# A two-layer decoder trunk: lo parts of 98 weight pieces subtracted by GpSimd instead of VectorE, in a new order of instructions

## The chip, the cores and the metric

One core of a Trainium2 chip runs the whole program. The metric is the device time of one execution in microseconds; the median of several runs is given, and one further execution was taken by the hardware profiler. The engines are called as the profile calls them: PE (TensorE, matmuls), PEld (its weight loads), DVE (VectorE), ACT (ScalarE), POOL (GpSimd), SP (SyncE, which issues most DMAs).

## The reference

Two layers over a sequence of 512 rows of 1024 float32 channels. Each layer normalises its input, multiplies it by one wide matrix, runs two branches, and merges them:

```python
h = rmsnorm(x, norm_g)
proj = h @ w_in                  # aq ak av az bqk bv bi bf bo bz ga gb
# branch A: differential attention, 8 heads, two score maps of 64 columns a head
q, k = rope(rmsnorm(aq)), rope(rmsnorm(ak))
a = softmax(q0 k0) - lam * softmax(q1 k1)     # causal
oa = rmsnorm(a @ v) * (1 - lam_init) * silu(az);   ya = oa @ w_out_a
# branch B: mLSTM matrix memory, 8 heads, causal convolution on q and k
hb = rmsnorm(mlstm(q, k, v, gates)) * sigmoid(bo) * silu(bz);   yb = hb @ w_out_b
u = sigmoid(ga) * ya + sigmoid(gb) * yb
x = x + u @ w_o
```

All of it is float32 in and out.

## The kernel before, in words

**Numbers in two parts.** PE multiplies in a rounded format (`fp32r`). To keep float32 accuracy every operand is split in a hi part and a lo part: ACT copies the source into the rounded format (`wh`, hi), and DVE subtracts that from the source (`wl`, lo). A product is then three matmuls: hi by hi, hi by lo, lo by hi. `split` does this for everything, weights and activations.

**Pieces.** The weights come from memory in pieces of 128 x 1024 values, 512 KB, in the order of `TUNE["order"]`: 111 pieces a layer, 222 in all. `qk0` to `qk3`, `av`, `bv` are four pieces each, `az`, `ga`, `bqk`, `bo`, `bz`, `woa`, `gb`, `wob` one for each index, `gate` is a small one, and `wo` is 14 pieces of a multiplication with seven products instead of eight (some of its weights are sums, which DMAs issued by POOL add up). `load` issues a piece's DMA on SP into one of two buffers `wr`; `prep`, three pieces ahead of the matmuls, makes `wh` (ACT) and `wl` (DVE), three buffers each. A piece is 24 matmuls of 512 columns.

**The rest of the work** hangs on clock ticks between pieces. In the first part of a layer the projections alternate with attention: `qk_done` normalises and rotates q and k (tiles `sq`, `rot`, `qss`), `back` transposes them in groups of four on PE (`qkt`) and ACT and DVE read them out (`qs`, `ks`, `kl`, or `qk_0x`, `qk_2x`); `attn_head` makes scores (`sc`), maxima (`mx`), probabilities (`p`), their transposes (`ut`) and the product with v. Later come the mLSTM heads (`ml_head`: `ms`, `dd`, `num`, `den`). The sums over 128 partitions that the norms need are matmuls with a matrix of ones: two of them (hi and lo), or one where `fold` first adds the two halves of the partitions and stacks hi and lo; `foldA`, `foldM`, `foldD` list the heads that fold. `qsq` lists the tiles whose squares are summed by ACT in eight 64-wide instructions; the others take one 512-wide square and a `tensor_reduce` on DVE. The tiles `sc`, `qk`, `qkt`, `ut`, `av` (as a matmul's output), `num`, `den`, `msp` lie in PSUM, the others in SBUF.

**The order of issue** is planned. `Recorder` records every operation with its dependences instead of issuing it, and `schedule` then plans all five queues with a cost for each operation, latencies between engines, the free buffers and a key for each operation (when it is due, with offsets by tile name in `bias`). The program is issued in that order, and each engine works through its own queue in order. The numbers in `TUNE` (`margin`, `pemargin`, `wait`, `wdiff`, `drain`, `risk`, `late` and others) are the planner's weights; `attn`, `ml`, `gateA`, `gct`, `gls`, `m4` and `acl` set the ticks at which steps fall due. All operations are issued from one helper, so the profile shows them under one line, L439, and is read by tile names.

The planner's cost of a POOL operation, and the place in `prep` where the pieces are split:

```python
if eng == "POOL":
    return 1000.0 if fn == "dma_start" else 200.0 + n
...
elif i < TUNE["wsp"]:
    A.copy(wh, loaded[i])
    for hf in range(2):
        cs = slice(S * hf, S * hf + S)
        V.tensor_tensor(wl[:, cs], loaded[i][:, cs], wh[:, cs].bitcast(F32), ALU.subtract)
else:
    split(wh, wl, loaded[i])
```

Of the kernel before, what the change touches and what calls it, by code (L numbers as in the profile page):

```python
# [9 lines left out]
F32 = mybir.dt.float32  # L10
# [3 lines left out]
ALU = mybir.AluOpType  # L14
# [21 lines left out]

TUNE = {
    "order": (
# [4 lines left out]
    ),  # L43
    "qkt": 5,
    "gct": 14,
    "gls": 6,
    "glf": 12,
    "attn": (1, 5, 5, 8, 9, 10, 12, 16, 16, 19, 24),
    "a0": 23,
    "ap": 18,  # L50
    "a4": 10,
    "ml": (1, 9, 11, 12, 13, 28),
    "ahead": 3,
    "lc": 9,
    "slack": 4130.0,
    "margin": 60.0,
    "pemargin": 48.4,
    "wait": 333.1,
    "swpen": 99746.2,
    "smargin": 0.2,  # L60
    "pwait": 2.0,
    "wdiff": 5762.0,
    "wsp": 0,
    "kact": (0, 2),
    "qsq": (1, 3),
    "foldA": (2, 3, 5, 6),
    "foldM": (0, 1, 2, 3, 4, 7),
    "foldD": (0, 1, 3, 5, 6),
    "warm": 18,
    "start": 'x0 ct ng w0 x1 w1 x2 x3',  # L70
    "prods": 'P1 P5 P3 P6 P2 P7 P4',
    "acl": 14,
    "gateA": 7,
    "gateM": 4,
    "actp": (0, 1, 2, 3),
    "m0": 217,
    "mp": 15,
    "m4": 17,
    "slots": 20,
    "bias": {'av': 11500.0, 'msp_a': -4400.0, 'wl': 2550.0, 'wo': -3700.0, 'mk': 6300.0, 'woh': -4650.0, 'wob': -850.0, 'bv': 2450.0, 'ht': 4400.0, 'woa': -1700.0, 'taz': -5550.0, 'sbo': -8700.0, 'wh': 7950.0, 'ga': -3100.0, 'ulZ': 7100.0, 'gt': -2650.0, 'qs': -5450.0, 'rq': -4050.0, 'p': -850.0, 'uz': -2750.0, 'x': -1750.0, 'ua': 5400.0, 'sdh': -3800.0, 'fo_b': -3100.0, 'lneps': 3350.0, 'wo1_P': 14300.0, 'qkt': -450.0, 'ml': 1700.0, 'den': -1900.0, 'sq': 3050.0, 'ulA': 10450.0, 'uhY': 1850.0, 'wo0_P': -850.0, 'cv': -2300.0, 'ulB': 8050.0, 'ob': 1850.0, 'gw': -150.0, 'out_0_dram': -3650.0, 'qss': 3500.0, 'gb': 100.0, 'xr': 1400.0, 'x1d': 5100.0, 'sinv': 5300.0, 'msl_a': 2200.0, 'p5_wo': -4150.0, 'saz': 3700.0, 's1_wo': 550.0, 'hh': -2400.0, 'mql': 1750.0, 'ulY': 9700.0, 'msp_b': 1200.0, 'em': -6750.0, 'sbz': -4900.0, 'wr': -2400.0, 'xn': 3500.0, 'posi': -500.0, 'ms': 12650.0, 'rot': 1400.0, 'sums': -1100.0, 'wt0_wo': 2350.0, 'mq': 650.0, 'uy': 100.0, 'qt': 5650.0, 'msh_d': 1700.0, 'gf': 1850.0, 'warm': -1450.0, 'ctab': 4550.0, 'gct': -4200.0, 'hl': 150.0, 'fo_a': 350.0, 'ones': 2100.0, 'fb_a': -700.0, 'ut': 450.0, 'ld': 5350.0, 'ang': -1900.0, 'mx': 5650.0, 'dq': 2300.0, 'uh': -500.0, 'gm': -550.0, 'fb_d': 1400.0, 'zeroc': 6400.0, 'gft': -100.0, 'bqk': 2050.0, 'gcol': -1000.0, 'oa': 500.0, 'sdl': 4250.0, 'uhB': 5750.0, 'tbz': 1150.0, 'cosv': 500.0, 'sc': 150.0, 'gi': 6100.0, 'msh_a': 400.0, 'uhA': 250.0, 'ss': 400.0, 'bo': 2500.0, 'posf': 2100.0, 'eps': -6650.0, 'fo_d': -2950.0, 'ws0_wo': -200.0, 'msh_b': -350.0, 'qk0_2x': 150.0, 'msl_d': -3500.0, 'junk': -900.0, 'epsc': 3000.0, 'fb_b': -100.0, 'kl': 1100.0, 'ks': -1450.0, 'msl_b': 200.0, 'ng': 550.0, 'rows': 150.0, 'gc': -150.0, 'qk1_0x': -500.0, 'qk1_2x': 100.0, 'stab': 650.0},  # L80
    "drain": 689.4,
    "risk": 335.5,
    "late": 278.0,
}


# [16 lines left out]
class Recorder:  # L103
# [111 lines left out]
    @staticmethod  # L215
    def cost(eng, fn, a, k):
        def cols(ap):
            n = 1
            for x in list(ap.shape)[1:]:
                n *= x  # L220
            return n

        def ps(ap):
            return isinstance(ap, bass.AP) and ap.space == PSUM

        n = cols(a[0])
        if eng == "PE" and a[0].tensor.name.startswith("warm"):
            return 350.0
        if eng == "PE":
            n = cols(a[2]) if fn == "matmul" else cols(a[0])  # L230
            return max(n / 2.4 + 13.4, 107.5)
        if eng == "POOL":
            return 1000.0 if fn == "dma_start" else 200.0 + n
        if eng == "ACT":
            x = 52 + n * 0.833 + (0 if ps(a[1]) else 42)
            for v in (k.get("bias"), k.get("scale")):
                if isinstance(v, bass.AP):
                    x += 93
            if k.get("accum_out") is not None:
                x += 93  # L240
            return x
        if eng == "DVE":
            aps = [v for v in a[1:] if isinstance(v, bass.AP)]
            if fn == "reciprocal":
                return 64 + 6.26 * n
            if fn == "memset":
                return 8 + n * 1.04
            if fn == "tensor_reduce":
                return 69 + cols(a[1]) / 0.96
            if fn == "tensor_tensor_scan":  # L250
                return 69 + 2 * n / 0.96
            fast = fn in ("tensor_scalar", "tensor_copy") and not ps(a[1])
            x = 69 + (n / 1.92 if fast else n / 0.96)
            if fn in ("tensor_scalar", "scalar_tensor_tensor"):
                x += 61 * sum(1 for v in a[2:] if isinstance(v, bass.AP) and cols(v) == 1)
            return x
        return 400.0
# [185 lines left out]
def kernel(ctx, tc, x, pos, wp, wg, cst, par, pb, ngb, out):  # L443
    nc = tc.nc
    depth = wp.shape[0]
# [28 lines left out]
    V, A, T = rec.engine("DVE", nc.vector), rec.engine("ACT", nc.scalar), rec.engine("PE", nc.tensor)  # L474
    SY = rec.engine("SP", nc.sync)
    G = rec.engine("POOL", nc.gpsimd)

    def t2(name, dt=F32):
        return s2.tile([P, S], dt, tag="s2", name=name)
# [7 lines left out]
    def split(hi, lo, src):  # L487
        A.copy(hi, src)
        V.tensor_tensor(lo, src, hi.bitcast(F32), ALU.subtract)
# [9 lines left out]
    ct = cp.tile([P, C_N], F32, name="ct")  # L499
    posi = cp.tile([P, NT], I32, name="posi")  # L500
# [10 lines left out]
    ones = cp.tile([P, P], F32R, name="ones")  # L511
    V.memset(ones.bitcast(F32), 1.0)
    epsc = cp.tile([P, 1], F32, name="epsc")
# [3 lines left out]
    lneps = cp.tile([P, 1], F32, name="lneps")  # L517
    V.memset(lneps, math.log(EPS))
    zeroc = cp.tile([P, 1], F32, name="zeroc")
    V.memset(zeroc, 0.0)  # L520

    rows = dram.tile([16, S], F32, name="rows")


    if TUNE["warm"]:
        pw = ps_acc.tile([P, S], F32, tag="acc", name="warm")
        zw = t2("zw", F32R)
# [5 lines left out]
    cosv = cp.tile([P, NT, 32], F32, name="cosv")  # L533
    sinv = cp.tile([P, NT, 32], F32, name="sinv")
# [71 lines left out]
    def give(n):  # L606
        state["q2"] -= n
# [13 lines left out]
    x1d = dram.tile([S, D], F32, name="x1d")  # L621
# [833 lines left out]
    pieces = [(l, e[1]) for l in range(depth) for e in layers[l][0]]  # L1455
# [6 lines left out]
    loaded, ready = {}, {}  # L1462
# [46 lines left out]
    def prep(i):  # L1509
        if i >= len(pieces) or i in ready:  # L1510
            return
        load(i)
        l, key = pieces[i]
        if key == "gate":
            wh = wpool.tile([P, 1024], F32R, tag="wh", name=f"wh{i}")
            w4 = wh.rearrange("p (k a n) -> p k a n", k=KT, a=2)
            split(w4[:, :, 0, :], w4[:, :, 1, :], loaded[i][:, :512].rearrange("p (k n) -> p k n", k=KT))
            ready[i] = (wh, None)
            return
        wh = wpool.tile([P, 1024], F32R, tag="wh", name=f"wh{i}")  # L1520
        wl = wpool.tile([P, 1024], F32R, tag="wl", name=f"wl{i}")
        if key[0] == "seven" and key[2] in ("P5", "P6", "P7", "P4"):
            _, n, prod, a = key
            load_sums(i)
            t = chains[n, a, 3] if prod == "P7" else chains[n, a]
            split(wh, wl, t)
            if prod in ("P5", "P6"):
                add_up(l, n, "T2" if prod == "P5" else "T4", a)
            else:
                give(1)  # L1530
        elif i < TUNE["wsp"]:
            A.copy(wh, loaded[i])
            for hf in range(2):
                cs = slice(S * hf, S * hf + S)
                V.tensor_tensor(wl[:, cs], loaded[i][:, cs], wh[:, cs].bitcast(F32), ALU.subtract)
        else:
            split(wh, wl, loaded[i])
        ready[i] = (wh, wl)

    for n in TUNE["start"].split():  # L1540
# [4 lines left out]
        else:  # L1545
            SY.dma_start(ng0 if n == "ng" else ct, ngb[0] if n == "ng" else cst)
    late_loads()
    prep(0)
    for i, run in enumerate(runs):
        if i in starts:  # L1550
# [94 lines left out]
```

## Time and profile before

| | |
|---|---|
| median of 3 runs | 1344.44 us (1344.25 to 1344.85) |
| the profiled execution's own time | 1344.67 us |
| its span, first to last instruction | 1342.9 us |
| PE busy | 1331.3 us |
| DVE busy | 1012.6 us |
| ACT busy | 904.7 us |
| POOL busy | 36.9 us, 44 instructions |
| granted TensorE clock | 0.999 |

The span is shorter than the execution's time by what lies around it. Busy times of different engines overlap, so they don't add up; an engine that is busy nearly all of the span leaves little that the others could give back. Rows of groups read: line, engine, operation, output <- inputs, shapes, count, then total busy us, mean ns of one, and the idle time before them with what ended it. Rows of the time line read: start us, duration us, engine, operation, and the idle time before it in brackets. Layer 0 runs to about 673 us, layer 1 from there.

### The profile page before, as it was taken

What the parts mean: (1) busy time and instruction counts of PE and PEld (TensorE: products, weight loads), DVE (VectorE), ACT (ScalarE), POOL (GpSimd) and SP (SyncE); (2) the same over time, 40 slices, a digit from 0 to 9 for tenths busy, and PEclk for the clock granted to TensorE, in tenths of its full rate; (3) what the DMA queues carried; (4) which work ended last, traced back from release to release, by engine and by line L of the source; (5) the groups of instructions that cost most, each with busy time, mean ns of one, the idle gap of its engine ahead of it and who ended that gap; (6) DMA issues with size and microseconds to landing.
All of it is one profiled execution on the core that took longest, in us unless ns stands there. A gap on an engine that the chain in (4) does not pass through costs nothing.

```text
span 1342.9 us, 17724 instructions
## 1 busy us (share of the span) xinstructions
PE 1331.3 (99%) x6300; PEld 1100.0 (82%) x6300; DVE 1012.6 (75%) x1806; ACT 904.7 (67%) x1828; POOL 36.9 (3%) x44
## 2 busy tenths in 40 slices
PE   8999999999999999999999999999999999999998
PEld 7787878888888888888888888788888888888887
DVE  7888988786549958755888888887754698587386
ACT  5787888885438858733668787888743488586243
POOL 1000000000000000000200000000000000000010
PEclk9999999999999999999999999999999999999999
DMA  5222222323244433455933122222322434434366
GB/s 186 87 79 64 79 78 64 94 77 101 91 119 112 132 108 114 137 136 146 265 104 97 53 95 63 79 63 94 99 82 91 120 107 135 128 109 140 121 190 172
DMA packets 51274, 148.17 MB, mean 110 GB/s; under 512 B 6096, under 2 KB 12880, under 8 KB 51184
## 3 DMA queue, kind: packets, MB, share of 16 engines
q1 hardware_dynamic: 48880, 138.63, 33.7%
q0 software_dynamic: 2304, 8.39, 3.5%
q8 instruction: 50, 0.82, 0.3%
q14 instruction: 40, 0.33, 0.1%
HBM read 142.74 MB, written 4.26 MB: 109 GB/s over the span
## 4 chain that ended last, share of the span: by engine, by line
PE 98%; ACT 1%; DMA 0%; DVE 0%; issue 0%; SPq 0%; DVEq 0%
PE qk L439 13%; PE av L439 9%; PE az L439 7%; PE ga L439 7%; PE bv L439 7%; PE bo L439 7%; PE bz L439 7%; PE woa L439 7%; PE gb L439 7%; PE bqk L439 7%; PE wob L439 6%; PE wo_P L439 6%; PE sc L439 3%; PE num L439 2%; PE ms L439 1%; PE ut L439 1%
## 5 line engine op out<-in xcount | busy, mean ns | idle before, releaser
L439 ACT CAST wh<-wr 128x1024 fp32r<-128x1024 f32 (+1 forms) x206 | 214.9, 1045 | 195.8 <-PE woa L439 37.7
L439 DVE TENSOR_TENSOR wl<-wr,wh 128x1024 fp32r<-128x1024 f32 x204 | 249.0, 1221 | 108.5 <-ACT wh L439 105.7
L439 PE MATMUL qk<-wl,hh 128*128 128x512 f32 x256 | 94.1, 398 | 0.7 <-DVE wl L439 0.7
L439 PE MATMUL qk<-wh,hl 128*128 128x512 f32 x256 | 93.8, 400 | 0.1
L439 PE MATMUL qk<-wh,hh 128*128 128x512 f32 x256 | 93.3, 399 | 0.6 <-ACT hh L439 0.6
L439 PE MATMUL woa<-oa,wh 128*128 128x512 f32 x256 | 88.5, 391 | 0.0
L439 PE MATMUL wob<-ob,wh 128*128 128x512 f32 x256 | 83.4, 389 | 0.0
L439 ACT ACTIVATE p<-sc,mx,rq 128x128 f32<-128x128 f32 (+3 forms) x128 | 78.9, 618 | 6.5 <-DVE mx L439 6.0
L438 ACT ACT_TABLE_LOAD x61 | 78.3, 1283 | 1.1
L439 PEld LDWEIGHTS qk<-wl,hh 128*128 128x128 f32 x256 | 47.9, 188 | 10.6 <-DVE wl L439 1.2
L439 PEld LDWEIGHTS wob<-ob,wh 128*128 128x128 f32 x256 | 48.1, 188 | 10.0
L439 PEld LDWEIGHTS qk<-wh,hl 128*128 128x128 f32 x256 | 48.0, 188 | 9.7 <-DVE hl L439 0.4
L439 PEld LDWEIGHTS woa<-oa,wh 128*128 128x128 f32 x256 | 47.8, 188 | 9.7
L439 PEld LDWEIGHTS qk<-wh,hh 128*128 128x128 f32 x256 | 47.7, 188 | 9.5 <-ACT hh L439 0.9
L439 DVE TENSOR_REDUCE mx<-sc 128x2 f32<-128x256 f32 (+1 forms) x64 | 52.5, 821 | 0.9
L439 PE MATMUL az<-hh,wl 128*128 128x512 f32 x128 | 51.3, 401 | 0.0
L439 PE MATMUL az<-hl,wh 128*128 128x512 f32 x128 | 50.9, 398 | 0.0
L439 PE MATMUL ga<-hh,wl 128*128 128x512 f32 x128 | 50.6, 398 | 0.0
L439 PE MATMUL ga<-hh,wh 128*128 128x512 f32 x128 | 50.5, 395 | 0.0
L439 PE MATMUL az<-hh,wh 128*128 128x512 f32 x128 | 50.5, 397 | 0.0
L439 PE MATMUL ga<-hl,wh 128*128 128x512 f32 x128 | 50.4, 394 | 0.0
L439 PE MATMUL woa<-oa,wl 128*128 128x512 f32 x128 | 50.0, 391 | 0.0
(314 smaller groups left out, 3737.7 us busy)
## 6 DMA issues: line engine op xcount, KB each, us to landing
wr<-in_wp_dram SPq DMA_DIRECT2D x204, 512.0 KB, 3.6
ws_wo<-in_wp_dram POOLq DMA_DIRECT2D x12, 512.0 KB, 6.6
dd<-rows SPq DMA_DIRECT2D x16, 256.0 KB, 4.9
em<-rows SPq DMA_DIRECT2D x16, 256.0 KB, 3.9
dd<-rows SPq DMA_DIRECT2D x16, 192.0 KB, 5.4
x<-in_x_dram SPq DMA_DIRECT2D x4, 512.0 KB, 8.5
dd<-rows SPq DMA_DIRECT2D x16, 128.0 KB, 6.2
ws_wo<-in_wp_dram SPq DMA_DIRECT2D x4, 512.0 KB
```

What stands on the lines that cost most here:

```text
L438: self.tc.keep_in_program_order(self.nc.scalar.preload_act_table_set(self.SET_NAME[o["load"]]))
L439: self.tc.keep_in_program_order(getattr(o["e"], o["fn"])(*o["a"], **o["k"]))
```

## The change

`prep` gets a branch: pieces 3 to 52 of each layer (49 of them are not the gate piece, which is split elsewhere) are copied by ACT as before, but the subtraction is issued to POOL. The planner's cost for such an operation is raised. `wsp` 3 makes the first three pieces of layer 0 use the existing branch that subtracts in two halves. One more head folds in each of `foldA`, `foldM` and `foldD`, `qsq` keeps one tile of four, and `order`, the ticks, the planner's weights and the table `bias` (from 114 names to 103, most values changed; left out here) are other ones.

```diff
     "order": (
-        "qk0 av0 gate az0 qk1 az1 az2 av1 qk2 az3 az4 qk3 ga0 az6 ga7 az5 ga3 ga2 ga4 az7 bv0 woa3 woa4 "
-        "bqk7 woa2 ga6 bqk4 bqk1 ga5 bo0 woa6 bo1 woa7 ga1 bz1 bqk5 bqk0 woa5 bz0 woa1 bqk6 woa0 bqk2 "
-        "bo2 bz2 bo4 bz4 bo3 bv1 bz3 bo6 bo5 bz5 bqk3 bo7 bz7 bz6 gb2 gb0 wob2 wob0 gb3 gb4 wob3 gb1 "
-        "wob1 gb6 gb7 wob6 wob4 gb5 wob5 wob7 wo"
+        "qk0 av0 gate az0 qk1 az1 az2 av1 qk2 az3 az4 qk3 az6 ga0 ga3 az5 ga2 ga4 ga7 az7 bv0 woa3 ga6 "
+        "bo0 woa4 bqk0 woa2 bqk7 bqk1 woa6 ga1 ga5 bo1 woa5 bz1 bqk5 bqk4 woa7 bz0 woa1 bqk6 woa0 bo2 "
+        "bz2 bo4 bz4 bqk2 bo3 bv1 bz3 bo6 bo5 bz5 bqk3 bo7 bz7 bz6 gb0 gb2 wob0 gb4 gb3 gb7 wob2 wob3 "
+        "wob4 gb6 gb1 wob6 wob1 gb5 wob5 wob7 wo"
     ),
-    "gct": 14,
-    "gls": 6,
+    "gct": 15,
+    "gls": 7,
-    "attn": (1, 5, 5, 8, 9, 10, 12, 16, 16, 19, 24),
+    "attn": (1, 5, 5, 9, 9, 10, 12, 16, 16, 19, 24),
-    "ml": (1, 9, 11, 12, 13, 28),
+    "ml": (1, 9, 10, 12, 13, 28),
-    "margin": 60.0,
-    "pemargin": 48.4,
-    "wait": 333.1,
-    "swpen": 99746.2,
-    "smargin": 0.2,
-    "pwait": 2.0,
-    "wdiff": 5762.0,
-    "wsp": 0,
+    "margin": 21.4,
+    "pemargin": 225.8,
+    "wait": 383.3,
+    "swpen": 8658.5,
+    "smargin": 101.0,
+    "pwait": 0.3,
+    "wdiff": 9165.4,
+    "wsp": 3,
-    "qsq": (1, 3),
-    "foldA": (2, 3, 5, 6),
-    "foldM": (0, 1, 2, 3, 4, 7),
-    "foldD": (0, 1, 3, 5, 6),
+    "qsq": (3,),
+    "foldA": (0, 1, 2, 5, 6),
+    "foldM": (0, 1, 2, 3, 4, 5, 7),
+    "foldD": (0, 1, 3, 4, 5, 6),
-    "acl": 14,
-    "gateA": 7,
+    "plo": (3, 50),
+    "acl": 12,
+    "gateA": 0,
-    "m4": 17,
+    "m4": 20,
-    "drain": 689.4,
-    "risk": 335.5,
-    "late": 278.0,
+    "drain": 508.6,
+    "risk": 41.0,
+    "late": 93.2,
...
         if eng == "POOL":
-            return 1000.0 if fn == "dma_start" else 200.0 + n
+            return 1000.0 if fn == "dma_start" else 200.0 + n * (2.0 if fn == "tensor_tensor" else 1.0)
...
+        elif len(pieces) // depth * l <= i - TUNE["plo"][0] < len(pieces) // depth * l + TUNE["plo"][1]:
+            A.copy(wh, loaded[i])
+            G.tensor_tensor(wl, loaded[i], wh.bitcast(F32), ALU.subtract)
         else:
             split(wh, wl, loaded[i])
```

More of the change, by code (lines that the diff above doesn't have):

```diff
@@ L77 @@
     "mp": 15,
-    "m4": 17,
+    "m4": 20,
     "slots": 20,
-    "bias": {'av': 11500.0, 'msp_a': -4400.0, 'wl': 2550.0, 'wo': -3700.0, 'mk': 6300.0, 'woh': -4650.0, 'wob': -850.0, 'bv': 2450.0, 'ht': 4400.0, 'woa': -1700.0, 'taz': -5550.0, 'sbo': -8700.0, 'wh': 7950.0, 'ga': -3100.0, 'ulZ': 7100.0, 'gt': -2650.0, 'qs': -5450.0, 'rq': -4050.0, 'p': -850.0, 'uz': -2750.0, 'x': -1750.0, 'ua': 5400.0, 'sdh': -3800.0, 'fo_b': -3100.0, 'lneps': 3350.0, 'wo1_P': 14300.0, 'qkt': -450.0, 'ml': 1700.0, 'den': -1900.0, 'sq': 3050.0, 'ulA': 10450.0, 'uhY': 1850.0, 'wo0_P': -850.0, 'cv': -2300.0, 'ulB': 8050.0, 'ob': 1850.0, 'gw': -150.0, 'out_0_dram': -3650.0, 'qss': 3500.0, 'gb': 100.0, 'xr': 1400.0, 'x1d': 5100.0, 'sinv': 5300.0, 'msl_a': 2200.0, 'p5_wo': -4150.0, 'saz': 3700.0, 's1_wo': 550.0, 'hh': -2400.0, 'mql': 1750.0, 'ulY': 9700.0, 'msp_b': 1200.0, 'em': -6750.0, 'sbz': -4900.0, 'wr': -2400.0, 'xn': 3500.0, 'posi': -500.0, 'ms': 12650.0, 'rot': 1400.0, 'sums': -1100.0, 'wt0_wo': 2350.0, 'mq': 650.0, 'uy': 100.0, 'qt': 5650.0, 'msh_d': 1700.0, 'gf': 1850.0, 'warm': -1450.0, 'ctab': 4550.0, 'gct': -4200.0, 'hl': 150.0, 'fo_a': 350.0, 'ones': 2100.0, 'fb_a': -700.0, 'ut': 450.0, 'ld': 5350.0, 'ang': -1900.0, 'mx': 5650.0, 'dq': 2300.0, 'uh': -500.0, 'gm': -550.0, 'fb_d': 1400.0, 'zeroc': 6400.0, 'gft': -100.0, 'bqk': 2050.0, 'gcol': -1000.0, 'oa': 500.0, 'sdl': 4250.0, 'uhB': 5750.0, 'tbz': 1150.0, 'cosv': 500.0, 'sc': 150.0, 'gi': 6100.0, 'msh_a': 400.0, 'uhA': 250.0, 'ss': 400.0, 'bo': 2500.0, 'posf': 2100.0, 'eps': -6650.0, 'fo_d': -2950.0, 'ws0_wo': -200.0, 'msh_b': -350.0, 'qk0_2x': 150.0, 'msl_d': -3500.0, 'junk': -900.0, 'epsc': 3000.0, 'fb_b': -100.0, 'kl': 1100.0, 'ks': -1450.0, 'msl_b': 200.0, 'ng': 550.0, 'rows': 150.0, 'gc': -150.0, 'qk1_0x': -500.0, 'qk1_2x': 100.0, 'stab': 650.0},
@@ L81 @@
-    "drain": 689.4,
-    "risk": 335.5,
-    "late": 278.0,
+    "bias": {'av': 15250.0, 'msp_a': -4100.0, 'wl': 2450.0, 'wo': -3700.0, 'woh': -4650.0, 'bv': 1500.0, 'woa': -4550.0, 'taz': -5950.0, 'sbo': -8700.0, 'wh': 9300.0, 'ga': -6750.0, 'ulZ': 10000.0, 'rq': -4500.0, 'uz': -3450.0, 'wo1_P': 11050.0, 'wo0_P': -2800.0, 'cv': -1950.0, 'p5_wo': -7600.0, 'mql': 3900.0, 'dd': 7450.0, 'gi': 11550.0, 'uy': 650.0, 'den': 15950.0, 'gct': -3150.0, 'oa': 3550.0, 'hl': 12400.0, 'ms_a': 4450.0, 'rot': 3700.0, 'dq': -5150.0, 'qs': -1650.0, 'sdl': -1100.0, 'gt': 400.0, 'xr': -5400.0, 'rn': -1750.0, 'sdh': 6450.0, 'mk': 5500.0, 'gw': 250.0, 'em': -5150.0, 'ul': -700.0, 'saz': 6900.0, 'bqk': -7400.0, 'fb_d': -100.0, 'num': 2650.0, 'qk0_2x': 1450.0, 'gf': -450.0, 'qk1_0x': 2400.0, 'warm': -550.0, 'pb': -10050.0, 'gcol': 850.0, 'zw': 700.0, 'gft': -850.0, 'fo_a': 4850.0, 'ld': 3100.0, 'gb': 100.0, 'ml': 1800.0, 'msh_a': -3150.0, 'p': -300.0, 'msh_b': -4400.0, 'ang': -4600.0, 'gc': -1200.0, 'ks': -2050.0, 's1_wo': -250.0, 'ws0_wo': 6450.0, 'mq': 3300.0, 'ulA': 500.0, 'msl_b': -3450.0, 'ht': -50.0, 'qy': 200.0, 'uh': 9750.0, 'par': -500.0, 'wt1_wo': -3300.0, 'msl_d': -3200.0, 'sq': -100.0, 'lq': -800.0, 'glf': 2350.0, 'sgb': 3200.0, 'mx': 3750.0, 'ms_b': 4950.0, 'ng': 550.0, 'qss': 400.0, 'qk0_0x': 200.0, 'junk': 2950.0, 'ob': -250.0, 'ss': -1400.0, 'out_0_dram': -2650.0, 'uhB': 150.0, 'sbz': 5100.0, 'uhY': 1550.0, 'cosv': -2950.0, 'rows': 200.0, 'ctab': 2400.0, 'msl_a': 200.0, 'wr': 1000.0, 'bo': 3250.0, 'ulY': -300.0, 'zeroc': 950.0, 'ct': -800.0, 'gm': -1150.0, 'epsc': -2850.0, 'bz': -100.0, 'eps': 200.0, 'sinv': 1050.0, 'qk1_2x': -2050.0},
```

## The prediction

> **What bounds the kernel now.** I read the page first: the share of each engine and the chain that ended last.
>
> ```profile
> span 1342.9 us, 17724 instructions
> PE 1331.3 (99%) x6300; PEld 1100.0 (82%) x6300; DVE 1012.6 (75%) x1806; ACT 904.7 (67%) x1828; POOL 36.9 (3%) x44
> PE 98%; ACT 1%; DMA 0%; DVE 0%; issue 0%; SPq 0%; DVEq 0%
> ```
>
> TensorE (PE) is busy 99% of the span and carries 98% of the chain. POOL has only 44 instructions. A busy share over the whole span can hide a stage with another limit, so I cut the span into stages. The columns are the stretch, its length, then the busy time of PE, PEld, DVE, ACT and POOL.
>
> ```profile
> 0.00:36.00 36.00, 32.63 (x143) 25.73 (x144) 26.48 (x71) 21.15 (x52) 4.94 (x9) 1.00 0.51 174
> 36.00:120.00 84.00, 82.95 (x415) 67.71 (x414) 75.31 (x176) 66.72 (x190) 0.95 (x1) 1.00 0.26 79
> 120.00:240.00 120.00, 118.64 (x594) 97.47 (x593) 103.75 (x228) 101.55 (x280) 1.90 (x2) 1.00 0.24 75
> 240.00:362.00 122.00, 122.00 (x590) 101.83 (x589) 83.44 (x145) 82.27 (x147) 1.90 (x2) 1.00 0.30 92
> 362.00:480.00 118.00, 118.00 (x544) 98.18 (x543) 86.57 (x119) 75.22 (x106) 1.90 (x2) 1.00 0.41 117
> ...
> 700.00:780.00 80.00, 79.41 (x397) 64.63 (x396) 70.77 (x159) 61.87 (x179) 0.95 (x1) 1.00 0.26 80
> 780.00:900.00 120.00, 118.63 (x596) 97.72 (x595) 104.58 (x234) 101.70 (x279) 1.90 (x2) 1.00 0.23 71
> ...
> 1260.00:1343.00 83.00, 79.00 (x347) 64.52 (x345) 52.62 (x74) 30.38 (x39) 5.18 (x6) 0.99 0.59 165
> ```
>
> PE idles 3.37 us in the first 36 us and 4.0 us in the last stretch. Between them it idles 1.05 + 1.36 + 0.59 + 1.37 = 4.37 us, all of it in the attention stretches of the two layers, where DVE is busy 86 to 90% of the time. Everywhere else PE never stops. The third view, one row of the groups by operation and four of the list of waits (us in total, times, longest), says what those 4.37 us are.
>
> ```profile
> L439 PE MATMUL qkt<-ct,rot 128*128 128x128 f32 x128 | 24.2, 278 | 4.4 <-ACT qk_2x L439 1.8 <-ACT qs L439 1.8 <-ACT qk_0x L439 0.5
> ...
> PE qkt L439 <- ACT qk_2x L439: 1.8, 4, 0.5
> PE qkt L439 <- ACT qs L439: 1.8, 4, 0.5
> ...
> PE qk L439 <- DVE wl L439: 0.7, 2, 0.4
> ...
> PE qkt L439 <- ACT qk_0x L439: 0.5, 1, 0.5
> ```
>
> All 4.4 us belong to the transposes qkt. The time line shows one of these waits:
>
> ```profile
> 187.61 0.49 PE L439 MATMUL qkt<-ct,rot 128*128 128x128 f32 x3
> 188.14 0.36 ACT L439 CAST qk_2x<-qkt 64x256 fp32r<-64x256 f32 x1 [0.81 <-PE qkt L439]
> 188.56 0.33 PE L439 MATMUL qkt<-ct,rot 128*128 128x128 f32 x1 [0.46 <-ACT qk_2x L439]
> ```
>
> Three transposes of a group of four run, ACT (which was idle) reads the first two, and the fourth transpose waits 0.46 us for that read. The order of issue puts the read ahead of the fourth transpose. The list has nine such waits, 0.49 us in the mean, in 128 / 4 = 32 groups. PE waits for a lo part of a weight (wl) only twice, 0.7 us, both in the first 15 us, and DVE is not what limits PE. Whatever the change saves on DVE, the PE time that can be had back is 4.4 us in the middle, part of 3.37 us at the start, and PE work that is removed.
>
> **The change part by part.**
>
> *1. Subtractions to GpSimd (`plo`).* 49 pieces a layer (50 less the gate piece), 98 in all, leave DVE:
>
> ```profile
> L439 DVE TENSOR_TENSOR wl<-wr,wh 128x1024 fp32r<-128x1024 f32 x204 | 249.0, 1221 | 108.5 <-ACT wh L439 105.7 <-PE bo L439 2.1
> ...
> L439 POOL MEMSET kl<- 64x1024 f32 x16 | 15.2, 948 | 320.0 <-PE sc L439 139.7 <-DVE sums L439 136.6 <-DVE junk L439 30.1
> ...
> L439 ACT CAST wh<-wr 128x1024 fp32r<-128x1024 f32 (+1 forms) x206 | 214.9, 1045 | 195.8 <-PE woa L439 37.7
> ...
> 25.01 0.39 PE L439 MATMUL qk<-wl,hh 128*128 128x512 f32 x1
> 25.24 0.39 PE L439 MATMUL qk<-wh,hl 128*128 128x512 f32 x1
> ...
> wr<-in_wp_dram SPq DMA_DIRECT2D x204, 512.0 KB, 3.6
> ```
>
> 98 x 1.221 = 119.7 us less for DVE; on the path that sets the end, 0, because PE does not wait for DVE there. The price of one subtraction on POOL is not in this trace. The nearest row is the memset, 948 ns for one pass over 1024 elements that only writes. A subtraction reads two streams and writes one: between 0.95 us (all at once) and 3 x 0.95 = 2.84 us (one after another). I take two passes, 1.9 us, since the two streams are what the memset lacks. The Trainium skill, GPSIMD Engine Reference, section 3.1, gives about 2.6 cycles an element for a two-input operation on this engine at 1.2 GHz, an estimate of 2.2 us here; no run shows it yet, the sum below is the same by it, and it raises the chance of the hold-up among the rivals.
>
> At 1.9 us, 49 subtractions are 93 us of POOL's time in some 330 us (139 us at 2.84): it keeps up. A load of raw weights waits on SP's queue for the subtraction that frees one of two raw buffers. A buffer's turn becomes 3.6 us to landing + 1.05 us ACT copy + 1.9 us = 6.6 us, for two buffers 3.3 us a piece. PE takes one matmul of 512 columns in 25.24 - 25.01 = 0.23 us, and a piece has 24: 5.5 us and whatever attention work lies between. The loads stay covered, as do the loads of `rows` queued behind them on SP. On POOL the subtractions stand behind the memsets of `kl` (0.95 us each), which wait for a free slot; the order is planned, so a memset should come to the front only about when its slot is free. The additions of `wo` by DMA come after piece 85 and meet none of them.
>
> What it costs if the cover is gone: the lead of a lo part over its first use.
>
> ```profile
> 189.37 1.23 DVE L439 TENSOR_TENSOR wl<-wr,wh 128x1024 fp32r<-128x1024 f32 x1
> 191.04 0.39 PE L439 MATMUL qk<-wl,hh 128*128 128x512 f32 x1
> ```
>
> Here the lead is 191.04 - 190.60 = 0.44 us, about the shortest there is. A POOL subtraction ends 0.7 us (at most 1.6 us) later and would hold PE for 0.3 to 1.2 us at such a place. But all places are planned anew, with the longer duration in the planner's cost line. I take 0 and keep this as a rival.
>
> *2. Three more folds a layer (`foldA`, `foldM`, `foldD`: 15 heads before, 18 after).* Each fold drops one of two 512-column matmuls with `ones`. What it adds has these rows:
>
> ```profile
> L439 DVE TENSOR_TENSOR ms_a<-ms_a,fb_a 64x512 f32<-64x512 f32 x8 | 5.4, 681 | 5.0 <-ACT fb_a L439 5.0
> L439 ACT ACTIVATE fb_a<-av 64x512 f32<-64x512 f32 x8 | 4.8, 596 | 0.1
> ```
>
> Three heads in two layers, 6 x 0.23 us = **-1.4 us**, straight off the bound. It adds 6 x 0.6 us on ACT and 6 x 0.68 us on DVE, and that much latency per head; in the attention stretches DVE's relief in part 1 hides it, and in the stretch of the mLSTM (362 to 480 us) PE is full with DVE at 73%. If it isn't hidden it gives the 1.4 us back.
>
> *3. `qsq` (1, 3) to (3,).* Eight tiles of 64-wide squares become one 512-wide square and a reduction on DVE.
>
> ```profile
> L439 ACT ACTIVATE sq<-qk 128x64 f32<-128x64 f32 x128 | 27.1, 227 | 2.3 <-PE qk L439 1.6
> L439 ACT ACTIVATE sq<-qk 128x512 f32<-128x512 f32 x16 | 9.5, 592 | 7.6 <-PE qk L439 7.5
> L439 DVE TENSOR_REDUCE qss<-sq 128x8 f32<-128x512 f32 x16 | 10.8, 676 | 2.7 <-ACT sq L439 2.7
> ```
>
> ACT loses 8 x (8 x 0.227 - 0.592) = 9.8 us at least, DVE gains 8 x 0.676 = 5.4 us. On PE: 0; the 119.7 us of relief cover DVE's part many times over.
>
> *4. `wsp` 0 to 3.* The first three pieces are subtracted in two halves, so PE can start on the first half.
>
> ```profile
> 9.39 1.23 DVE L439 TENSOR_TENSOR wl<-wr,wh 128x1024 fp32r<-128x1024 f32 x1 [1.50 <-ACT wh L439]
> 10.67 0.50 PE L439 MATMUL qk<-wl,hh 128*128 128x512 f32 x1 [0.27 <-DVE wl L439]
> 14.58 0.50 PE L439 MATMUL qk<-wl,hh 128*128 128x512 f32 x1 [0.41 <-DVE wl L439]
> ```
>
> These two waits (0.7 us) shrink; the next thing PE lacks is the following transposed input, also late here. I take **-0.4 us**, between 0 and -0.7.
>
> *5. The new order of pieces, steps and issue (`order`, `attn`, `ml`, `gateA`, the planner's weights).* The pieces and their matmuls are the same, so PE's work is unchanged; only waits are drawn anew. The 9 late transposes are what there is to lose; the bounds are 0 of 32 groups (-4.4 us) and 32 of 32 (32 x 0.49 - 4.4 = +11.3 us). Each arose where ACT stood idle for want of input (0.81 us in the row above). ACT's inputs in these stretches come largely from DVE, which is now a fifth emptier, so ACT should have other work ready more often. I take half: **-2.2 us**.
>
> **Sum.** -1.4 - 0.4 - 2.2 = -4.0 us. The profiled execution took 1344.67 us, 1342.9 of span and 1.77 around it, and 0.23 above the median of the runs, 1344.44. So 1344.44 - 4.0 = **1340.4 us**. With every gain at its best (-1.4 - 0.7 - 4.4) it is 1337.9: the rest is PE work. A change of 0.2%, 2.7 us, is about what a measurement of this kernel can tell from none: faster begins at 1341.8, slower at 1347.1.
>
> **The rivals.**
>
> *No change.* The waits redrawn come out as many as before: -1.4 - 0.4 gives 1342.6, and some new waits of 0.5 us bring it to about 1343. For it: nothing in the code removes the pattern of the fourth transpose, and PE never waited for what part 1 relieves. Against it: less DVE load in just those stretches.
>
> *POOL and DVE hold each other up (slower).* While POOL reads its two streams, DVE instructions that read two SBUF tiles might stand still. From 36 to 240 and 700 to 900 us DVE is idle 8.7 + 16.2 + 9.2 + 15.4 = 49.5 us, and these rows show what it loses of subtractions there:
>
> ```profile
> 36.00:120.00 84.00, 13.45 (x12) 1.00 0.26 79
> 120.00:240.00 120.00, 20.65 (x17) 1.00 0.24 75
> 700.00:780.00 80.00, 13.45 (x11) 1.00 0.26 80
> 780.00:900.00 120.00, 20.05 (x17) 1.00 0.23 71
> ```
>
> 67.6 us by 57 subtractions. DVE becomes the bound when one subtraction on POOL holds it up by more than (67.6 + 49.5) / 57 = 2.05 us. At 1.9 us it isn't; at 2.84 us it would cost 0.79 x 57 = 45 us; between the two, at 2.37 us, 0.32 x 57 = 18 us: 1344.4 - 1.8 + 18 = 1361. Against it: a DVE instruction that reads PSUM (`sc`, `qk`, `qkt`, `ut`) has one SBUF input at most, so not every subtraction can hold DVE for its full length, and POOL's memsets show nothing of it. The Trainium skill, SBUF — State Buffer, section "Who interferes with whom", states such a rule: a Vector instruction with two SBUF inputs contends with a GpSimd instruction that reads SBUF, and whichever is second waits until the first is done. With the 2.2 us of the other page it would cost 0.15 x 57 = 8.6 us, 1351, if every subtraction held DVE for all its length. No GpSimd instruction of this trace reads SBUF, so the trace neither bears it out nor speaks against it.
>
> *Late lo parts (slower).* If POOL's results come late at places with leads as short as the one above, each costs up to 1.2 us. Six places gain 7 us against the 1.8 us of parts 2 and 4: about 1349. It decides from four places on.
>
> **How the numbers follow.** Forecast 0.50 (1337.9 to 1341.7), no change 0.28, hold-up 0.12, late lo parts 0.10. So faster 0.50, same 0.28, slower 0.22. The range runs from 1337.5 to 1350: it leaves out most of the hold-up and a little below the best sum.
>
> **What would show it.** Groups: 98 subtractions `wl<-wr,wh` on POOL with a mean near 1.9 us, on DVE 103 whole ones and six halves; six matmuls with `ones` fewer. Waits: the PE row of qkt near 2.2 us instead of 4.4. Stages: PE idle below 4.4 us between 36 and 1260 us, DVE at some 70% in the attention stretches. The hold-up would show as DVE instructions with two SBUF inputs longer than their rows of today (`rot<-rot,sq`, `p<-p,sums`); late lo parts as PE waiting for POOL `wl`. The forecast is wrong if the late transposes grow in number, or if PE waits for POOL at four places or more.

## The result, and the profile after

The changed kernel takes **1420.38 us** (1417.64 to 1422.91) beside 1344.35 us of the kernel before on the same chip: a ratio of 1.0564, with a 95% interval of 1.0540 to 1.0589. It is 76 us slower where 4 us less was forecast. The profiled execution took 1422.31 us. Its page, and the mean granted clock of the core (0.999 before):

```profile
span 1420.5 us, 17678 instructions
...
PE 1354.6 (95%) x6294; PEld 1106.8 (78%) x6294; DVE 1005.6 (71%) x1725; ACT 898.4 (63%) x1714; POOL 275.6 (19%) x142
...
PE 71%; DVE 19%; ACT 6%; issue 2%; DMA 1%; SPq 0%; DVEq 0%; ACTq 0%
```

```profile
core 0: 1420.5 us, clock 0.989
```

Two lines carry the surprise. DVE lost 98 subtractions of 1.22 us, 119.7 us of work, and gained some 10 us (step 3 and the folds), so it should stand near 902 us; it stands at 1005.6. About 100 us of DVE time have come from nowhere. And DVE now has 19% of the chain that ended last, where it had 0%. The span grew by 77.6 us: PE idle (span less PE busy) went from 11.6 to 65.9 us, which is 54.3, and PE's busy time rose by 23.3 us although six matmuls are gone. Part of that second term is the clock: 0.989 instead of 0.999 over 1420 us is an estimate of 14 us of full-speed time at most, since a low clock costs nothing where PE idles. The rest is not broken down.

The stages of layer 0, and one stretch of layer 1 (columns as in the prediction: PE, PEld, DVE, ACT, POOL, then granted clock, DMA share, GB/s):

```profile
36.00:120.00 84.00, 74.75 (x345) 58.74 (x344) 64.39 (x138) 54.21 (x136) 26.60 (x12) 0.96 0.19 60
120.00:240.00 120.00, 108.38 (x527) 86.62 (x526) 97.34 (x193) 86.56 (x220) 38.29 (x18) 0.99 0.22 67
240.00:362.00 122.00, 112.50 (x548) 91.53 (x547) 83.90 (x158) 88.91 (x193) 41.66 (x19) 0.99 0.24 71
362.00:480.00 118.00, 118.00 (x535) 98.26 (x534) 67.47 (x89) 56.56 (x79) 17.30 (x9) 1.00 0.37 109
480.00:600.00 120.00, 120.00 (x559) 100.44 (x558) 96.09 (x138) 93.19 (x131) 0.00 (x0) 1.00 0.45 124
...
800.00:920.00 120.00, 107.25 (x527) 84.82 (x527) 100.86 (x205) 84.89 (x216) 41.09 (x19) 1.00 0.21 67
```

PE idles 30.4 us between 36 and 362 us, where attention runs and POOL subtracts. From 362 to 480 us POOL still works (17.3 us) and PE doesn't stop for a moment; from 480 to 600 us POOL does nothing and PE is full. So the loss lies where subtractions on POOL meet attention, not wherever POOL is busy.

The subtractions themselves, in the view of one tile (minimum, median and maximum in ns, then first and last start in us):

```profile
L440 POOL TENSOR_TENSOR wl<-wr,wh x98: 2368/2400/2927, 26.5 to 1092.3; 128x1024 fp32r<-128x1024 f32 x98
```

The median is 2.40 us, between the bounds 0.95 and 2.84 and above the 1.9 us taken. No row of the waits has PE waiting for a `wl` of POOL. What did grow are rows of DVE whose instructions nobody changed. Before, then after:

```profile
L439 DVE TENSOR_TENSOR kl<-qkt,ks 64x256 fp32r<-64x256 f32 x32 | 13.4, 420 | 4.0 <-ACT ks L439 3.2
...
L439 DVE TENSOR_TENSOR sums<-sums,ml 128x2 f32<-128x2 f32 x64 | 10.1, 158 | 1.7
...
L439 DVE SCALAR_TENSOR_TENSOR mx<-mx,rq 128x2 f32<-128x2 f32 x64 | 10.0, 156 | 1.2
...
L439 DVE TENSOR_TENSOR fo_a<-ms_a,fo_a 64x512 fp32r<-64x512 f32 x8 | 5.5, 685 | 1.7 <-ACT fo_a L439 1.6
```

```profile
L440 DVE SCALAR_TENSOR_TENSOR mx<-mx,rq 128x2 f32<-128x2 f32 x64 | 25.9, 405 | 1.1
...
L440 DVE TENSOR_TENSOR sums<-sums,ml 128x2 f32<-128x2 f32 x64 | 22.5, 351 | 1.7
...
L440 DVE TENSOR_TENSOR fo_a<-ms_a,fo_a 64x512 fp32r<-64x512 f32 x10 | 20.2, 2017 | 2.5 <-ACT fo_a L440 2.4
...
L440 DVE TENSOR_TENSOR kl<-qkt,ks 64x256 fp32r<-64x256 f32 x32 | 13.4, 420 | 7.7 <-ACT ks L440 7.4
```

An instruction on two columns (`mx`) went from 156 to 405 ns in the mean; `kl`, which reads one input from PSUM, kept its 420 ns exactly. The mean hides what happens to the single one. The time line:

```profile
152.05 4.79 POOL L440 TENSOR_TENSOR wl<-wr,wh 128x1024 fp32r<-128x1024 f32 x2 [6.86 <-ACT wh L440]
...
152.17 2.34 DVE L440 SCALAR_TENSOR_TENSOR mx<-mx,rq 128x2 f32<-128x2 f32 x1
...
154.54 0.43 DVE L440 TENSOR_TENSOR kl<-qkt,ks 64x256 fp32r<-64x256 f32 x1
...
155.11 0.30 PE L440 MATMUL ut<-ct,p 128*128 128x128 f32 x1 [1.49 <-DVE kl L440]
```

POOL starts two subtractions in a row at 152.05. `mx` starts 0.12 us later and, instead of 0.16 us, takes 2.34: until 154.51, about the end of the first subtraction (152.05 + 2.40 = 154.45). `kl` stands behind it on DVE's queue, and PE stands 1.49 us in front of a transpose that is due after `kl`. Of the 64 `mx`, 12 are long in this way; all ten `fo_a` are. Counted instruction by instruction against its undisturbed duration, 70 DVE instructions are lengthened by more than 60 ns, by 99.0 us together and by 2.25 us at most. That is the missing time of DVE.

Which ones they are is seen by their inputs. All 70 began while a subtraction was running on POOL. Of the instructions that began so, with at least 0.1 us of the subtraction left, those with two inputs in SBUF were lengthened almost without exception: 10 of 10 `sums<-sums,ml`, 10 of 10 `fo_a`, 8 of 8 `p<-p,sums`, 12 of 13 `mx` (the thirteenth began in the same moment as the subtraction). With one input in SBUF, none was of 13 `sums<-sums` (a reciprocal) or of 10 `ul<-ut,uh` (the other input lies in PSUM). One row with one SBUF input and a number, `qt<-qt`, goes with the first kind (3 of 3).

The longest rows of PE's waits are now these; `msp_a`, `ut` and `av` had next to none before:

```profile
PE msp_a L440 <- DVE ul L440: 7.7, 6, 1.4
PE ut L440 <- DVE kl L440: 6.3, 4, 1.6
PE ut L440 <- DVE ul L440: 4.9, 4, 2.1
PE qkt L440 <- DVE kl L440: 4.5, 4, 1.2
PE av L440 <- DVE saz L440: 3.7, 4, 1.4
```

### The profile page after: what moved, and what is told of

It reads as the page before. It is cut to its first block, busy times and chain, and to the rows that moved or that the text cites. A ratio compares the mean times of both kernels' runs of the same rounds, so it can differ in the third digit from the quotient of the medians.

```text
span 1420.5 us, 17678 instructions
## 1 busy us (share of the span) xinstructions
PE 1354.6 (95%) x6294; PEld 1106.8 (78%) x6294; DVE 1005.6 (71%) x1725; ACT 898.4 (63%) x1714; POOL 275.6 (19%) x142
## 4 chain that ended last, share of the span: by engine, by line
PE 71%; DVE 19%; ACT 6%; issue 2%; DMA 1%; SPq 0%; DVEq 0%; ACTq 0%
PE woa L440 6%; PE bz L440 6%; PE gb L440 6%; PE bo L440 6%; PE bqk L440 6%; PE qk L440 6%; PE wob L440 5%; PE bv L440 5%; PE ga L440 5%; PE av L440 4%; PE wo_P L440 4%; DVE rot L440 3%; DVE mx L440 2%; PE num L440 2%; PE sc L440 2%
## 5 line engine op out<-in xcount | busy, mean ns | idle before, releaser
L440 POOL TENSOR_TENSOR wl<-wr,wh 128x1024 fp32r<-128x1024 f32 x98 | 238.6, 2441 | 534.9 <-ACT wh L440 410.2
L440 DVE TENSOR_TENSOR wl<-wr,wh 128x1024 fp32r<-128x1024 f32 (+1 forms) x109 | 129.5, 1192 | 92.6 <-ACT wh L440 92.3
L440 PE MATMUL qk<-wh,hh 128*128 128x512 f32 x256 | 98.2, 412 | 0.8 <-ACT hh L440 0.8
L440 PE MATMUL qk<-wl,hh 128*128 128x512 f32 x256 | 97.9, 409 | 0.5 <-DVE wl L440 0.5
L440 PE MATMUL qk<-wh,hl 128*128 128x512 f32 x256 | 97.2, 409 | 0.1
L440 POOL DMA_DIRECT2D ws_wo<-in_wp_dram x12 | 10.6, 879 | 372.0 <-DMA ws_wo<-in_wp_dram 286.1
L440 PE MATMUL wob<-ob,wh 128*128 128x512 f32 x256 | 79.3, 389 | 0.0
L440 DVE SCALAR_TENSOR_TENSOR p<-p,sums 128x128 f32<-128x128 f32 (+1 forms) x64 | 48.7, 761 | 8.3 <-ACT p L440 7.7
L440 ACT ACTIVATE p<-p,sums 128x128 f32<-128x128 f32 (+1 forms) x64 | 36.0, 563 | 25.3 <-DVE sums L440 25.1
```

The lines of the kernel that those rows point to most:

```text
L440: self.tc.keep_in_program_order(getattr(o["e"], o["fn"])(*o["a"], **o["k"]))
```

## The experiments

Theory A: DVE is held while POOL reads its two SBUF streams, and PE waits for the chains behind the held instructions. Theory B: the new order of issue is slow by itself. The diffs are against the changed kernel unless said otherwise. Where the expectations speak of some 107 us of lengthening, the count instruction by instruction gives 99.0.

**Is it the order, or the subtraction on POOL?** `e3_before_pool` is the kernel before with nothing but the branch in `prep` and the cost line:

```diff
+    "plo": (3, 50),
-            return 1000.0 if fn == "dma_start" else 200.0 + n
+            return 1000.0 if fn == "dma_start" else 200.0 + n * (2.0 if fn == "tensor_tensor" else 1.0)
+        elif len(pieces) // depth * l <= i - TUNE["plo"][0] < len(pieces) // depth * l + TUNE["plo"][1]:
+            A.copy(wh, loaded[i])
+            G.tensor_tensor(wl, loaded[i], wh.bitcast(F32), ALU.subtract)
```

> The kernel before with one thing alone from the change: the branch that gives pieces 3 to 52 of each layer to POOL, and the planner's cost for it; all other settings are the old ones. Theory A: most of the 76 us appear, 1390 to 1430, and the same DVE instructions lengthen. Rival B: near 1344, at most 1355.

1430.95 us, ratio 1.0641 [1.0625, 1.0657]: a hair above the range of A. The subtraction on POOL alone makes a loss of 86 us; the rest of the change is not needed for it. (This kernel is planned anew too; the 10 us by which it loses more than the change are about what another order alone can make, see `e12_redraw_more` below.) Here 81 DVE instructions are lengthened by 96.8 us, and `mx` even to 671 ns:

```profile
L440 DVE SCALAR_TENSOR_TENSOR mx<-mx,rq 128x2 f32<-128x2 f32 x64 | 42.9, 671 | 1.1
```

`e4_pool_writes` keeps the order and keeps POOL as busy, but lets it read almost nothing: two subtractions of 16 columns with memsets between.

```diff
+            if o["eng"] == "POOL" and o["fn"] == "tensor_tensor":
+                w, r, h, op = o["a"]
+                keep(g.tensor_tensor(w[:, 0:16], r[:, 0:16], h[:, 0:16], op))
+                for c0, c1 in ((16, 1008), (16, 1008), (16, 300)):
+                    keep(g.memset(w[:, c0:c1].bitcast(F32), 0.0))
+                keep(g.tensor_tensor(w[:, 1008:1024], r[:, 1008:1024], h[:, 1008:1024], op))
+                continue
```

> The changed kernel with its planned order; on POOL each subtraction is replaced at its place by a subtraction of the first 16 columns, memsets of the middle of wl, and a subtraction of the last 16 columns, about 2.4 us together. The lo parts of the middle columns are left out (zero). POOL is as long busy and wl is as late as in the changed kernel, the waits for wh and the hold on the raw buffer stay, but POOL reads SBUF only for a moment at either end. Theory A: DVE instructions with two SBUF inputs are at their old lengths apart from short blocks, time 1338 to 1352. Rival C (POOL's longer latency, its queue and late buffers cost the time, not DVE's block): 1410 to 1425. Theory A2 (DVE is blocked by POOL's writes too): in between or as slow as the change.

1346.24 us, ratio 1.0010 [1.0000, 1.0019]: as A has it. Same order, same wait for the copies, POOL busier than in the changed kernel, DVE as empty as it was meant to be, and the loss is gone.

```profile
PE 1334.0 (99%) x6294; PEld 1099.9 (82%) x6294; DVE 913.8 (68%) x1725; ACT 897.1 (67%) x1714; POOL 290.2 (22%) x534
```

It shows a second thing: with DVE relieved by about 100 us for nothing, this order still doesn't beat the kernel before. Its rows of waits of `qkt`:

```profile
PE qkt L449 <- ACT qs L449: 1.1, 4, 0.4
...
PE qkt L449 <- ACT qk_2x L449: 0.9, 2, 0.5
...
PE qkt L449 <- ACT qk_0x L449: 0.5, 1, 0.5
```

**The same work on DVE, unplanned and planned.** `e1_same_order_dve` issues each of the 98 subtractions on DVE, at the place in the order that was planned for POOL. `e2_replan_dve` gives POOL no pieces, so that the planner knows.

```diff
+            e = self.nc.vector if o["eng"] == "POOL" and o["fn"] == "tensor_tensor" else o["e"]
+            self.tc.keep_in_program_order(getattr(e, o["fn"])(*o["a"], **o["k"]))
```
```diff
-    "plo": (3, 50),
+    "plo": (3, 0),
```

> The changed kernel with its own planned order on every engine, but each of the 98 subtractions that stood in POOL's queue is issued at its place to DVE instead. Theory A (a subtraction on POOL blocks DVE instructions that read two SBUF tiles or run in a doubled mode): the blocked time, some 107 us, goes and 119.7 us of subtractions come onto DVE, which the plan did not count; mx<-mx,rq falls from 405 to about 156 ns and fo_a<-ms_a,fo_a from 2017 to about 685; time between 1345 and 1375. Rival B (the new order of pieces, steps and issue is what costs, wherever the subtraction runs): still 1410 or more.

> The changed kernel with no piece given to POOL (plo 50 to 0), planned anew with all its other settings: order of pieces, ticks, folds, qsq, wsp, planner's weights. Theory A: 1338 to 1346, near the kernel before, with DVE's two-SBUF instructions at their old lengths. Rival B (the new settings are bad by themselves): 1380 to 1420.

e1: 1387.72 us, 1.0318 [1.0303, 1.0332], between the two expectations, so a miss. e2: 1346.54 us, 1.0014 [1.0005, 1.0023], half a microsecond above its range. In e1 `mx` is back at 155 ns and only 1.2 us of lengthening is left in all, so DVE is not held; but it has 119.7 us of work that its order doesn't know, and that costs 1387.7 - 1346.5 = 41 us, with waits of the same kind:

```profile
PE qkt L441 <- DVE kl L441: 5.8, 8, 1.2
```

By e4 and e2, each beside the kernel before on its own chip (1344.6 us), the new settings with all their other edits are worth +1.6 and +1.9 us: no gain, and no loss of the size that B needs. The two also differ by the 119.7 us of subtractions that DVE has in e2 and not in e4, and by 0.3 us of time: relief of DVE is worth next to nothing here. Late transposes are fewer in e2 as well, with no relief of DVE:

```profile
PE qkt L440 <- ACT qk_0x L440: 0.9, 2, 0.5
```

**Does the hold end with the POOL instruction?** `e5_quarters` makes four subtractions of 256 columns out of each.

```diff
+                for c in range(0, 1024, 256):
+                    cs = slice(c, c + 256)
+                    self.tc.keep_in_program_order(self.nc.gpsimd.tensor_tensor(w[:, cs], r[:, cs], h[:, cs], op))
```

> The changed kernel with its planned order, each POOL subtraction issued as four of 256 columns one after another. Theory A1 (the block is for the whole instruction that came first, so a DVE instruction waits at most for the rest of the running piece): no wait over about 0.65 us, the 107 us of lengthening on DVE fall to 25 to 45 us, the longest mx<-mx,rq from 2.4 us to under 0.9 us; time 1355 to 1380. Rival A3 (POOL's reading takes the second reader away from DVE as long as POOL has work, however it is cut): lengthening near 107 us again and 1410 or more.

1366.57 us, 1.0161 [1.0142, 1.0181]: within the range. POOL needs more time in all (302.1 us instead of 238.6), yet the loss falls from 76 to 22 us. The longest lengthening falls from 2.25 to 0.61 us, its sum from 99.0 to 43.9 us, now over 119 instructions:

```profile
L444 POOL TENSOR_TENSOR wl<-wr,wh 128x256 fp32r<-128x256 f32 x392 | 302.1, 804 | 417.5 <-ACT wh L446 283.2 <-ACT ld L446 56.7 <-issue 47.3
```

A DVE instruction can thus start between two short POOL instructions, where it has to wait for the end of a long one.

**Half of the pieces.** `e7_half` sends 48 subtractions to POOL instead of 98 (`"plo": (3, 25)`).

> The changed kernel with 25 pieces a layer to POOL instead of 50 (pieces 3 to 27), planned anew. Theory A: the loss goes with the number of subtractions that stand beside attention, about half of 76 us: 1370 to 1395. If a few critical places made the loss: under 1360 or over 1410.

1396.78 us, 1.0387 [1.0373, 1.0401], 2 us above the range. Half the pieces keep 59.6 of the 99.0 us of lengthening and 52 of the 76 us: by these numbers the earlier half of them costs twice what the later half adds (24 us), though e7 is planned anew and some of the difference can be its order.

**Can the order be planned around it?** `e6_block_planned` gives the planner the measured 2.4 us and a rule: a POOL subtraction and a DVE operation with no input in PSUM (of four kinds: `tensor_tensor`, `scalar_tensor_tensor`, `tensor_scalar`, `tensor_copy`) don't overlap. `e10_quarters_planned` adds the quarters.

```diff
+            return max(s, held[other[e]]) if shares[i] else s
...
+            if shares[i]:
+                held[e] = s + c
```

> The changed kernel with the block written into the planner: a DVE instruction whose tensor inputs all lie in SBUF (two of them, or one in a tensor_scalar) isn't planned beside a POOL subtraction, nor the other way round, and a subtraction is costed at 2400 ns. All queues are planned anew with it; the work is the same. Theory D (the block costs PE so much because every queue's order was fixed without it: PE stands in front of an instruction that the plan had ready): most of the 76 us come back, 1346 to 1375, with the DVE lengthening still there or smaller. Rival E (the blocked DVE time itself is what PE lacks, planned or not): 1400 or more.

> The kernel e6_block_planned (block written into the planner) with each subtraction issued as four of 256 columns, 3.2 us together where the plan has 2.4. If both measures act on the same blocked time, one after the other: DVE lengthening 15 to 30 us and 1352 to 1368, the best of the versions with POOL, still slower than before. If the pieces' longer total (0.8 us more each) takes it back: over 1370.

e6: 1381.21 us, 1.0286 [1.0261, 1.0312], between the expectations, a miss for both: half of the loss is avoided. The planned order leaves 45.0 us of lengthening over 38 instructions; those that are left are as long as before (up to 2.22 us). e10: 1366.66 us, 1.0163 [1.0148, 1.0178], within its range but no better than the unplanned quarters. A plan that knows the rule still meets it; that the engines don't keep the plan's times is a likely reason that no run shows.

**Are delays on DVE enough?** `e9_delays` is e4 with idle DVE work (a `reciprocal` or a `memset` on a spare tile) ahead of the same 70 instructions, each about as long as that instruction was lengthened in the changed kernel: 90.5 + 6.1 = 96.6 us inserted.

```diff
+            if o["eng"] == "DVE":
+                left = DELAYS.get(count, 0)
+                count += 1
+                if left > 270:
+                    n = min(256, int((left - 150) / 6.2))
+                    self.tc.keep_in_program_order(self.nc.vector.reciprocal(self.idle[:, 0:n], self.idle[:, 0:n]))
```

> The kernel e4_pool_writes (same planned order as the change; POOL writes instead of subtracting, lo parts of the middle columns left out) with idle work put on DVE: in front of each of the 70 DVE instructions that the change's trace shows lengthened by over 60 ns, a reciprocal or memset on a scratch tile of the length by which that very instruction was lengthened there, 99 us in all (at most 2.0 us each). Theory A (DVE's late results alone make the loss): 1405 to 1425, with PE's idle time and its half-speed stretches back. Rival F (POOL's reads also slow something else, ACT, PE or the transfers): under 1385.

1402.84 us, 1.0432 [1.0414, 1.0449], 2 us below the range of A and far above the other. Over e4 that is 56.6 us, 56.6 / 74.1 = 76% of the loss, from delays alone, with almost no read of POOL behind them (the two subtractions of 16 columns). The waits come back too, nearly in the same order:

```profile
PE ut L464 <- DVE kl L464: 5.2, 4, 1.3
PE msp_a L464 <- DVE ul L464: 4.9, 6, 1.0
```

The other 17.5 us are not settled. The granted clock was 0.995 to 0.997 in the four runs here and 0.989 to 0.994 in those of the changed kernel; in the means, 0.996 and 0.991, that is an estimate of 7 us at most. Nothing separates the rest (delays cut at the tile's size, POOL held by DVE in its turn).

**The folds, and what a new order is worth.** `e8_before_folds` is the kernel before with only the three lists `foldA`, `foldM`, `foldD` of the change. `e11_redraw` and `e12_redraw_more` are the kernel before with one planner's weight moved, `"slack"` from 4130 to 4140 and to 4300, and no work changed.

> The kernel before with the three lists of folding heads from the change and nothing else: six matmuls of 512 columns fewer on PE, six ACT and six DVE instructions more. The prediction's step 2: -1.4 us, 1343.0. Rival: the longer way to the mean (one more ACT and one more DVE instruction a head) or the order planned anew makes new waits for PE, 1345 or more.

> The kernel before with one weight of the planner, slack, 4130 to 4140 ns, and no change in the work: the same operations in an order planned anew. If 1353 of e8_before_folds came from an order drawn anew rather than from the folds' own cost, this lies several us above the kernel before too, 1347 to 1360. If the order hardly depends on such a weight: 1344 to 1346, and the folds' longer way is what cost e8 its 9 us.

> The kernel before with slack 4130 to 4300 ns and no change in the work. The order that comes out differs from before about as much as that of e8_before_folds does (2763 lines of PE's queue against 2242; in e11_redraw it was 34). If the 9 us of e8 came from drawing the order anew: 1348 to 1360. If they are the folds' own cost: 1343 to 1346.5.

e8: 1353.46 us, 1.0064 [1.0050, 1.0078]; the rival held. e11: 1344.63 us, 1.0000 [0.9990, 1.0009], but its order differs from that of before in only 34 lines of PE's queue, so it tells nothing. e12: 1352.90 us, 1.0061 [1.0044, 1.0077], with as much of PE's queue reordered as in e8. So 8.5 us come from another order alone, and e8's 9 us need no cost of folding; nor do they show that folding gains.

**All of them beside each other.** Lengthening is the sum over DVE's instructions of their duration over the undisturbed one of the same shape, where more than 60 ns.

| kernel | lengthening us (instructions) | longest us | PE idle us | over before us |
|---|---|---|---|---|
| changed | 99.0 (70) | 2.25 | 65.9 | 76.0 |
| e3, before + POOL only | 96.8 (81) | 2.21 | 69.1 | 86.4 |
| e7, half | 59.6 (39) | 2.21 | 47.9 | 52.2 |
| e6, hold planned | 45.0 (38) | 2.22 | 38.2 | 36.6 |
| e5, quarters | 43.9 (119) | 0.61 | 22.2 | 22.0 |
| e10, quarters planned | 28.6 (71) | 0.61 | 23.5 | 22.1 |
| e4, POOL writes | 9.0 (16) | 0.85 | 10.5 | 1.6 |
| e2, all on DVE | 1.2 (2) | 0.67 | 13.0 | 1.9 |

The kernels with whole subtractions lose 0.8 to 0.9 us for each us of lengthening, those in quarters 0.5 to 0.8. Only e4 and e5 keep the changed kernel's order; the others are planned anew, so up to some 9 us of a difference between two rows can be the order's (e12). The four runs of e5 lie in two pairs, 1362.8 and 1363.9 us at a granted clock of 1.000 and 1369.3 and 1369.4 at 0.996, so its tie with e10 is no closer than that. None beats the kernel before.

## Why the prediction was wrong

- **The step that failed is part 1's "on the path that sets the end, 0".** It counted what DVE loses (119.7 us) and what POOL needs, and took for granted that DVE's other instructions keep their durations. DVE lost those 119.7 us and got 99.0 back as lengthening.
- **The hold-up was named, and its price was the second error.** That rival was worked out by DVE's load: DVE becomes the bound when one subtraction holds it for more than 2.05 us. Measured, a subtraction held it for 99.0 / 98 = 1.0 us on average, half of that threshold, and it cost 76 us instead of nothing. A DVE that is 71% busy (77 and 81% in the stretches from 36 to 240 us) is not the bound; the held instructions lie in chains that PE reaches in a fixed order (at 155.11 us it stands before a transpose while `kl` waits behind `mx`), and e9 shows that delays of that size at those places cost 57 us with DVE at 71%. The rival should have been priced by how far the held chains run ahead of PE, against a hold of up to one subtraction, not by a share of the load. The leads of those chains were not read; the one lead that the prediction did read, 0.44 us for a lo part, is a fifth of a hold of 2.3 us. By that argument it comes out slower at 1.9 us already, and 0.12 was too small a chance.
- **What spoke "against it" did hold**: rows that read PSUM kept their durations (`kl` 420 and 420 ns). It only wasn't enough. The rule of the Trainium skill, SBUF — State Buffer, section "Who interferes with whom", that a Vector instruction with two SBUF inputs and a GpSimd instruction reading SBUF wait for each other, is borne out: the trace agrees, with 0.16 us turned into 2.34 for `mx`, and in the other direction with a subtraction of 2.93 us that began at 210.28 us, 0.01 us after `msl_a<-ms_a,msh_a` on DVE. e4 takes nearly all the reads away and with them the lengthening, from 99.0 to 9.0 us.
- **The size of one subtraction**: 2.40 us, not the 1.9 taken; within the bounds. The Trainium skill, GPSIMD Engine Reference, section 3.1, led to an estimate of 2.2 us, nearer than mine. It would have changed the hold-up's price and not the sum.
- **Late lo parts** did not come: PE never waits for a `wl` of POOL. The places were planned anew with 2.25 us in the cost line, as part 1 argued.
- **Step 2** (-1.4 us): the six matmuls are gone (6300 to 6294), but the gain can't be seen; an order drawn anew moves this kernel by 8.5 us (e12).
- **Step 3** (0): nothing measured speaks against it. **Step 4** (-0.4): nothing gained. PE still waits 0.5 us for a `wl` of DVE and 0.8 for the next transposed input near the start (0.7 and 0.6 before).
- **Step 5** (-2.2): the size came by luck. In e4 the late transposes are 1.1 + 0.9 + 0.5 = 2.5 us instead of 4.4, a gain of 1.9. But the reason given, an emptier DVE that feeds ACT, is not borne out: in e2 DVE keeps its subtractions and these waits are 0.9 us. How many transposes come late is drawn with the order. (The 0.49 us a wait is 4.4 / 9; the nine listed waits are 4.1 us, 0.46 each.) Nor does the gain show in the time: e4 is 1.6 us slower than before although its PE idles less, 10.5 us instead of 11.6, because PE's busy time rose by 2.7 us. In its first 36 us the granted clock was 0.95, where it had been 1.00, an estimate of 0.05 x 36 = 1.8 us of it at most. "No change" was the true value, within 2 us, of everything in this edit but the subtractions.
- **Not foreseen at all** is the clock. It was 0.989 to 0.994 in the four runs, 0.999 before: over 1420 us an estimate of 7 to 14 us of the loss at most.

## What to carry to other kernels

Before work is moved to an engine that looks idle, ask which instructions of the other engines it can hold, and price that by the slack of the chain they are in: one 0.16 us instruction held for 2.3 us costs PE what its lead doesn't cover, whatever the load of its engine is. Relief of an engine that the bound doesn't wait for is worth nothing here (e4 beside e2), so even a small risk on the other side decides. If such work must go there, short instructions help more than a plan (quarters 22 us, planned whole ones 37), and in a kernel whose order is planned, a gain under 9 us can't be told from the order drawn anew unless an experiment draws it anew without the edit.

## What the runs showed of the hardware that was not expected

- A DVE instruction on 128 x 2 values, 156 ns undisturbed, took 2.34 us beside a POOL subtraction; each of the 70 long ones ended 0.13 to 0.20 us less than its normal duration after the subtraction did, so the shortest end about with it.
- POOL's subtraction of fp32 took 2400 ns for 1024 columns, 740 for 256 and 248 for 16: about 2.1 ns a column, and 0.2 us for the instruction itself.
- POOL that only writes also holds some of DVE. In e4, by the view of the tile `qt` (minimum, median, maximum in ns), an instruction with one SBUF input and a number took up to 1012 ns (154 to 176 before), which is more than a 16-column subtraction lasts and about a memset (928), and each of the five lengthened ones ended 0.03 us after a memset did; its neighbour with two SBUF inputs of the same size took 191 at most:

```profile
L449 DVE TENSOR_TENSOR qt<-qy x16: 161/172/191, 37.8 to 893.9; 128x16 f32<-128x16 f32 x16
...
L449 DVE TENSOR_SCALAR qt<-qt x16: 156/175/1012, 39.2 to 895.3; 128x16 f32<-128x16 f32 x16
```

- The granted clock can fall where PE idles: in the stretch from 36 to 120 us, where PE idled 9.25 us (the longest wait of the whole execution is 3.6 us), it was 0.96, where it had been 1.00. The sum of idle time alone doesn't do it: in e1 PE idled 42.9 us, in waits of at most 1.6 us, and the mean clock was the 0.999 of the kernel before.

```profile
core 0: 1386.2 us, clock 0.999
```

In e2 one wait of 1.62 us, at 121.6 us, stands shortly ahead of a stretch at about half speed (0.57 from 124 to 128 us). No run here separates what decides.
